# Two projections of a decoder trunk made block by block while scale and shift are still being computed

## The chip, the core and the metric

The kernel runs on one core of a Trainium2 chip. The metric is device time in microseconds; before the change the median of three runs is 1387.54 us (1387.46 to 1388.73). The engines are TensorE (PE, with its weight loads PEld), VectorE (DVE), ScalarE (ACT), GpSimd (POOL) and SyncE (SP, which here only issues transfers). Instructions of one engine run in the order in which the planner has put them.

## The reference, cut to what matters

One decoder layer for 576 tokens (512 of a prompt, 64 of eight samples), 1024 channels. Everything in this document happens in its first lines:

```python
ada = jax.nn.silu(c) @ w_ada + b_ada              # c: 9 rows
sh1, sc1, g1, sh2, sc2, g2 = jnp.split(ada, 6, axis=-1)
xm = x * (1.0 + sc1) + sh1                        # scale and shift, per sequence
proj = xm @ w_in                                  # 1024 -> 9228, cut into branches
u, v, ga, gg, pin, zz, xbc, dtr, gl = jnp.split(proj, IN_SPLIT_IDX, axis=-1)
h = ga * jax.nn.sigmoid(gg)                       # branch B: gate, then a convolution of 31 taps
```

The four branches, a gated merge, two layer norms and a mixture of 32 experts follow; they are not touched.

## The kernel before, in words

All activations lie with channels on partitions: `xT` is 8 blocks of 128 channels by 576 tokens. Products are made in split precision: each fp32 operand is a high part rounded to fp32r and a low part. ScalarE rounds (`cast`, line 316), VectorE subtracts (`lo`, line 322), and `prod` (line 581) makes high x high, high x low and low x high. One projection of 128 columns is 8 blocks x 3 x 2 halves of 288 tokens = 48 matmuls (line 589) into one `mm` tile in PSUM; there are two `mm` tiles.

**Weights.** `plan_front` (line 507) lists every weight tile in the order of use, and `Pipe` loads them in that order on SP's queue into a ring of buffers (`fill`, line 215). A kind `w1` tile (512 KB, for scale and shift) is used as it is; a `ct` tile (512 KB, for one projection) is split when one is asked for by `get` (line 280): `get` splits all that are loaded while fewer than four split ones lie unused. A split carries a high priority (line 257). The first eight `w1` tiles lie in buffers of the split weights, the other eight in buffers of their own (`r0`), the `ct` tiles in four `raw` buffers; so 20 loads are issued at the start, 16 `w1` and four `ct`, and between them, by hooks, the eight blocks of `xT` (288 KB each, after every second `w1`) and the small tensors `prm`.

**Scale and shift** go block by block, here called turns 0 to 7. `rows(k)` (line 427) takes two `w1` tiles and makes scale and shift of block k as nine rows, in 32 matmuls of the profile (line 434); ScalarE copies them to `adr` (line 438). `cols(k)` (line 440) turns them into columns on TensorE (line 446), VectorE adds the bias (line 447), ScalarE scales and shifts the prompt's tokens of the block (line 450), POOL those of the samples, and VectorE makes the high part `xh` (line 453) and the low part `xl` (line 454). `cols` and the copy carry a high priority, so `cols(k)` comes right behind `rows(k)`.

**Branch B** comes next. `b_step(j)` (line 693) makes projection `gg` (`pg`), takes its sigmoid into `sg` on ScalarE (line 704), makes projection `ga` (`pa`), and VectorE multiplies them into `ebp` and `ebs` (lines 706 to 708). From then on the convolution can start: 31 taps of block j on VectorE (line 720), those of the samples on POOL (lines 727 to 732). The taps wait in a list from which `step` takes so many behind each product. `ebp` and `ebs` take up space that `xT` and the other tiles of the start have left.

**The order.** The program says what comes first; a planner (`schedule_with_timeline_sim`) then puts each engine's instructions in order by its own estimate of when they are ready, and among ready ones takes the one with the higher priority, by default the one that was written first. So an instruction may come ahead of earlier ones that wait.

Of the kernel before, what the change touches and what calls it, by code (L numbers as in the profile page):

```python
# [176 lines left out]
NH, NR = 4, 4  # L177
# [13 lines left out]
BME = lambda nc: nc.vector  # L191
HP0 = 2000
N0 = 8
GA = 4
NL = 7
GM = (1, 1, 1, 1, 1)
# [111 lines left out]
class K:  # L308
# [64 lines left out]
    def build(s):  # L373
        nc, A, tc, ctx = s.nc, s.A, s.tc, s.ctx
        s.pse = ExitStack()
        s.ps = s.pse.enter_context(s.pool("ps", space=PSUM))
        con = ctx.enter_context(s.pool("con", side="left"))
        s.con = con
        ring = ctx.enter_context(s.pool("ring", side="left"))
        M = s.M = ExitStack()  # L380
        mp = M.enter_context(s.pool("M", side="left"))
        X = s.X = ExitStack()
        xp = X.enter_context(s.pool("X", side="left"))
        s.cst = con.tile([128, C_N], F32, name="cst")
        s.prm = con.tile([128, P_N], F32, name="prm")
        x0 = ExitStack()
        stp = x0.enter_context(s.pool("start", side="right"))
        cT = stp.tile([128, 8, 9], F32, name="cT")
        bT = stp.tile([128, 16], F32, name="bT")
        nc.scalar.dma_start(cT, A["cT"])  # L390
        nc.scalar.dma_start(bT, A["ba1"])
        nc.scalar.dma_start(s.cst, A["cst"])
        s.plan_front()
        s.ring = ring
        s.pipe = Pipe(s, s.plan, ring, NH, lambda i: (ring, "hi" if i < NH else "lo") if i < 2 * NH else
                      (stp, "r0") if i < 16 else (ring, "raw"), {"raw": NR, "r0": N0, "hi": NH, "lo": NH})
        xT = stp.tile([128, 8, NT], F32, name="xT")
        for k in range(8):
            s.pipe.hook[2 * k + 1] = lambda k=k: nc.sync.dma_start(xT[:, k], A["xT"][:, k])
        s.pipe.hook[16] = lambda: nc.sync.dma_start(s.prm, A["prm"])  # L400
        s.pipe.fill()
        eps = con.tile([128, 1], F32, name="eps")
        nc.vector.memset(eps, EPS)
        s.eps = eps
        s.dram = ctx.enter_context(s.pool("scr", space=bass.MemoryType.DRAM))

        zz = stp.tile([128, 513], F32, name="zz")
        nc.vector.memset(zz, 0.0)
        nc.scalar.activation(zz[:, 512:], eps, AF.Silu)
        p = s.ms()  # L410
        for _ in range(NW):
            nc.tensor.matmul(p[:9], zz[:, :9], zz[:, :512], start=True, stop=True)

        sil = s.sil = con.tile([128, 8, 32], F32, name="sil")
        nc.gpsimd.memset(sil, 0.0)
        nc.scalar.activation(sil[:, :, :9], cT, AF.Silu)
        s.adad = s.dram.tile([9, 4096], F32, name="adad")
        nc.gpsimd.dma_start(s.adad, A["bada"].to_broadcast([9, 4096]))
        b1 = bT.rearrange("p (k v) -> p k v", v=2)[:, :, 0]
        nc.vector.tensor_scalar(b1, b1, 1.0, None, op0=OP.add)  # L420
        scsh = stp.tile([128, 8, 2, 9], F32, name="scsh")
        xh = xp.tile([128, 8, NT], FR, name="xh")
        xl = xp.tile([128, 8, NT], FR, name="xl")
        s.xh, s.xl = xh, xl
        adr = {}

        def rows(k):

            p = s.ms()
            for v in range(2):  # L430
                w = s.pipe.take(2 * k + v)
                for i in range(8):
                    g = 32 * (i % 4)
                    nc.tensor.matmul(p[g:g + 32, v * 128:(v + 1) * 128], sil[:, i], w[:, i * 128:(i + 1) * 128],
                                     start=(i < 4), stop=(i >= 4), skip_group_check=True)
            adr[k] = stp.tile([128, 256], F32, name="adr", tag="adr", bufs=3)
            with tc.high_priority(offset=HP0):
                nc.scalar.copy(adr[k], p[:, :256])

        def cols(k):  # L440

            r = adr.pop(k)
            q = s.ms()[:, :18].rearrange("p (v r) -> p v r", r=9)
            with tc.high_priority(offset=HP0):
                for v in range(2):
                    nc.tensor.matmul(q[:, v], r[:, v * 128:(v + 1) * 128], s.cc("m9"), start=True, stop=True)
                nc.vector.tensor_tensor(scsh[:, k], q, bT[:, 2 * k:2 * k + 2].unsqueeze(2).to_broadcast([128, 2, 9]), OP.add)
                sc, sh = scsh[:, k, 0], scsh[:, k, 1]
                xs = xT[:, k, TP:].rearrange("p (b t) -> p b t", t=8)
                nc.scalar.activation(xT[:, k, :TP], xT[:, k, :TP], AF.Identity, bias=sh[:, 0:1], scale=sc[:, 0:1])  # L450
                nc.gpsimd.tensor_tensor(xs, xs, sc[:, 1:9].unsqueeze(2).to_broadcast([128, 8, 8]), OP.mult)
                nc.gpsimd.tensor_tensor(xs, xs, sh[:, 1:9].unsqueeze(2).to_broadcast([128, 8, 8]), OP.add)
                nc.vector.tensor_copy(xh[:, k, :], xT[:, k, :])
                s.xlast = nc.vector.tensor_tensor(xl[:, k, :], xT[:, k, :], xh[:, k, :].bitcast(F32), OP.subtract)
        for k in range(8):
            rows(k)
            if k:
                cols(k - 1)
        cols(7)
        x0.close()  # L460
        merged = mp.tile([128, 8, NT], F32, name="merged")
        s.merged = merged


        s.stk = []

        def opn(name, side):
            e = ExitStack()
            p = e.enter_context(s.pool(name, side=side))
            s.stk.append(e)  # L470
            return p, e
        s.opn = opn
        s.wk, s.wke = opn("wk", "left")
        s.bp, be = opn("bp", "right")
        s.cp, ce = opn("cp", "right")
        for j in range(4):
            s.b_step(j)
            s.step(7, s.anchor)
        for g in range(4):
            s.c_step(g)  # L480
            s.step(2.0, s.anchor)
        s.gates("C", 2, 4, lambda: s.yC, first=True, budget=6.0)
        ce.close()
        s.yAp, ye = opn("yAp", "left")
        s.ap, ae = opn("ap", "right")
        s.a_u()
        s.a_v()
        s.flush()
        ae.close()
        s.gates("B", 1, 4, lambda: s.yB, budget=6)  # L490
        be.close()
        s.dp1, s.d1e = opn("dp1", "right")
        s.dp, d2e = opn("dp", "right")
        s.dpa, dae = opn("dpa", "right")
        s.d_proj()
        s.flush()
        dae.close()
        s.dpb, dbe = opn("dpb", "right")
        s.ssd_queue()
        s.gates("A", 0, 4, lambda: s.yA, budget=BA)  # L500
        s.cond_rows()
        ye.close()
        if any(fn is None for c, fn, a in s.bg):
            s.flush(True)
        s.de = (dbe, d2e)

    def plan_front(s):
        A = s.A
        pl = []
        for i in range(16):  # L510
            pl.append(("w1", A["wa1"][i], 1024))
        for i in range(12):
            pl.append(("ct", A["wct"][i], 1024))

        def gates(k, w, kt):
# [32 lines left out]
        def add(nm, ap):  # L548
            if len(s.mi) == GA:
                s.wag = len(pl)  # L550
# [27 lines left out]
                               start=(hs[0] == 0), stop=(hs[0] > 0), skip_group_check=True)  # L578
        return p

    def prod(s, p, wh, wl, off, kt, h, l, m=128):

        nc = s.nc
        for k in range(kt):
            a, b = wh[:, off + k * m:off + (k + 1) * m], wl[:, off + k * m:off + (k + 1) * m]
            for n, (w, x) in enumerate(((a, h), (a, l), (b, h))):
                for hf in range(2):
                    xk = x[k] if isinstance(x, list) else x[:, k]
                    nc.tensor.matmul(p[:m, hf, :288], w, xk[:, hf * 288:(hf + 1) * 288],  # L589
                                     start=(k == 0 and n == 0), stop=(k == kt - 1 and n == 2))  # L590

    def ctile(s):
        wh, wl = s.pipe.get("ct")
        p = s.mm()
        s.prod(p, wh, wl, 0, 8, s.xh, s.xl)
        return p
# [676 lines left out]
    def build2(s):  # L1273
# [72 lines left out]
        for i in range(base, len(s.plan)):  # L1346
            m = s.mi.get(i, -1)
            if m < 0 or len(seq) < GA:
                t = (s.ring, "raw") if n9 % (NR + NB) < NR else (s.raw2, "rb")
                n9 += 1  # L1350
                if seq and m < 0:
                    late.append(t)
            elif len(seq) < GA + len(late):
                t = late[len(seq) - GA]
            else:
                t = seq[-(GA + len(late))]
            tags[i] = t
# [662 lines left out]
```

## Time and profile before

| | us |
|---|---|
| median of three runs | 1387.54 |
| the profiled execution, its own time | 1388.56 |
| its span, first to last instruction | 1386.7 |
| TensorE busy | 1309.0 |
| VectorE busy | 776.7 |
| ScalarE busy | 408.8 |
| GpSimd busy | 320.4 |

The profile is one execution. Times in it are counted from the first instruction. A line of the timeline gives start and duration in us, engine, line of the kernel, operation, output <- inputs with shape, how many were merged (xN), and in brackets how long the engine was idle before and what ended that. A matmul's duration overlaps that of its neighbours, so the pace is read from starts. PEclk is the clock that TensorE was granted, as a share of 2.4 GHz.

### The profile page before, as it was taken

Reading aid. Unit: us, or ns where it says so; the run is one execution under the profiler, and the core shown is the slowest. Engines: PE = TensorE matmul, PEld = TensorE weight load, DVE = VectorE, ACT = ScalarE, POOL = GpSimd, SP = SyncE. Lnnn points to the kernel's source line nnn. Section 1 sums busy time; section 2 is a strip of 40 time slices with the busy share of each in tenths; the row PEclk is TensorE's granted clock in tenths of the full one; section 3 lists DMA queues with packets and bytes.
Section 4 is the critical chain, followed back from the end, with each engine's and each line's share of the span. In section 5 each row is a group of like instructions: output and inputs, shape, how many; then the busy total and the mean of one; then the engine's idle time right before and its main releaser. Section 6 shows DMA issues by size and latency. Waiting matters only on the chain. (4 is left out here: it accounts for less than half of the span.)

```text
span 1386.7 us, 20311 instructions
## 1 busy us (share of the span) xinstructions
PE 1309.0 (94%) x7962; PEld 944.1 (68%) x7962; DVE 776.7 (56%) x1333; ACT 408.8 (29%) x657; POOL 320.4 (23%) x335
## 2 busy tenths in 40 slices
PE   7997899999999999999999987999999999999992
PEld 5997899999999877788899863344334444444331
DVE  3799797572676356667524487244444334434347
ACT  3311222642463424556422332021111111111114
POOL 1796004051321315333333151000000000000003
PEclk6998999999999989899999997999999999999997
DMA  9522123222322354361222969899999999999972
GB/s 378 151 76 61 54 92 110 69 69 84 108 77 84 113 200 170 129 230 43 72 85 93 320 241 358 340 414 414 414 415 414 415 413 415 414 415 415 415 296 99
DMA packets 90376, 318.15 MB, mean 229 GB/s; under 512 B 11113, under 2 KB 11265, under 8 KB 90271
## 3 DMA queue, kind: packets, MB, share of 16 engines
q1 hardware_dynamic: 83176, 293.29, 55.6%
q0 software_dynamic: 6528, 22.63, 4.8%
q8 instruction: 63, 1.03, 0.3%
q10 hardware_dynamic: 576, 0.93, 0.2%
q14 instruction: 33, 0.27, 0.1%
HBM read 307.16 MB, written 9.78 MB: 229 GB/s over the span
## 5 line engine op out<-in xcount | busy, mean ns | idle before, releaser
L1746 PE MATMUL mh<-raw,xg 128*64 128x512 f32 x1024 | 247.7, 605 | 0.2 <-DMA raw<-in_we_dram 0.2
L589 PE MATMUL mm<-xh,wh 128*128 128x288 f32 x1088 | 244.0, 305 | 2.9 <-DVE ebs L708 2.4
L589 PE MATMUL mm<-xh,wl 128*128 128x288 f32 x1088 | 240.4, 302 | 2.1 <-DVE wl L322 2.1
L589 PE MATMUL mm<-xl,wh 128*128 128x288 f32 x1088 | 240.4, 301 | 0.0
L316 ACT CAST wh<-raw 128x1024 fp32r<-128x1024 f32 (+3 forms) x120 | 113.1, 948 | 316.5 <-PE mm L589 228.3
L322 DVE TENSOR_TENSOR wl<-raw,wh 128x1024 fp32r<-128x1024 f32 (+3 forms) x112 | 133.3, 1194 | 130.1 <-ACT wh L316 129.7
L589 PEld LDWEIGHTS mm<-xh,wh 128*128 128x128 f32 x1088 | 180.9, 194 | 5.7 <-issue 3.3
L589 PEld LDWEIGHTS mm<-xh,wl 128*128 128x128 f32 x1088 | 178.8, 192 | 4.8 <-DVE wl L322 3.2
L589 PEld LDWEIGHTS mm<-xl,wh 128*128 128x128 f32 x1088 | 179.2, 193 | 0.4 <-issue 0.3
L1746 PEld LDWEIGHTS mh<-raw,xg 128*64 128x64 f32 x1024 | 75.2, 138 | 132.8 <-issue 117.4
L1793 DVE TENSOR_TENSOR x<-x,mc 128x512 f32<-128x512 f32 x120 | 78.2, 682 | 124.3 <-PE mc L1732 124.3
L1703 PE MATMUL mh<-raw,h 128*64 128x512 f32 x512 | 130.2, 601 | 1.0 <-ACT h L1761 0.7
L1670 POOL DMA_INDIRECT gr<-xmd,idi x16 | 16.2, 1010 | 415.9 <-PE mh L1746 385.4
L720 DVE SCALAR_TENSOR_TENSOR acc<-ebp,prm,acc 128x512 f32<-128x512 f32 x120 | 104.9, 883 | 2.1
L1703 PEld LDWEIGHTS mh<-raw,h 128*64 128x64 f32 x512 | 40.4, 136 | 72.0 <-issue 56.6
L1715 ACT CAST yh<-y 128x512 fp32r<-128x512 f32 x32 | 19.8, 620 | 220.9 <-DVE y L1714 207.4
L632 POOL TENSOR_TENSOR merged<-merged,sg 128x576 f32<-128x576 f32 x23 | 43.2, 1877 | 108.9 <-DVE sg L631 108.8
L1714 DVE SCALAR_TENSOR_TENSOR y<-mh,ws,G 128x512 f32<-128x512 f32 x32 | 24.0, 751 | 70.2 <-PE mh L1703 70.2
L1732 PEld LDWEIGHTS mc<-yh,ohT 128*128 128x128 f32 x120 | 22.4, 187 | 52.1 <-issue 47.1
L1732 PE MATMUL mc<-yh,ohT 128*128 128x512 f32 x120 | 53.6, 447 | 0.0
L1750 ACT ACTIVATE sg<-mh 128x512 f32<-128x512 f32 x16 | 9.6, 597 | 128.5 <-issue 78.6
L1732 PE MATMUL mc<-yl,ohT 128*128 128x512 f32 x120 | 47.4, 395 | 0.0
(436 smaller groups left out, 2010.3 us busy)
## 6 DMA issues: line engine op xcount, KB each, us to landing
raw<-in_we_dram SPq DMA_DIRECT2D x384, 512.0 KB
raw<-in_wa_dram SPq DMA_DIRECT2D x48, 512.0 KB
raw<-in_wct_dram SPq DMA_DIRECT2D x36, 512.0 KB
raw<-in_wgl_dram SPq DMA_DIRECT2D x32, 512.0 KB
raw<-in_wo_dram SPq DMA_DIRECT2D x16, 512.0 KB
raw<-in_wbr_dram SPq DMA_DIRECT2D x24, 256.0 KB
s<-in_st_ssm_dram POOLq DMA_DIRECT2D x4, 768.0 KB, 4.8
out_ssms_dram<-s POOLq DMA_DIRECT2D x4, 768.0 KB, 4.7
```

Of the source, the lines that this page charges most:

```text
L316: r = s.nc.scalar.copy(out, in_)
L322: r = (s.nc.gpsimd if pool else s.nc.vector).tensor_tensor(out, full, hi, OP.subtract)
L589: nc.tensor.matmul(p[:m, hf, :288], w, xk[:, hf * 288:(hf + 1) * 288], start=(k == 0 and n == 0), stop=(k == kt - 1 and n == 2))
L632: (nc.vector if nm == "D" and d == 7 else nc.gpsimd).tensor_tensor(m, m, sg, OP.add)
L720: nc.vector.scalar_tensor_tensor(o, i, wt, o, op0=OP.mult, op1=OP.add)
L1670: s.glast = nc.gpsimd.indirect_dma_start(out=gr[:n], out_offset=None, in_=s.xmd[:, :], in_offset=bass.IndirectOffsetOnAxis(ap=ix[:n, 0:1], ...
L1703: s.dlast = s.pe(nc.tensor.matmul(p[r], h[:, f, r], ws[o][:, kk * 512:(kk + 1) * 512], start=(f == 0), stop=(f == 3), skip_group_check=True))
L1714: V.scalar_tensor_tensor(y, p, ws, s.G2[0][:, hf * 512:hf * 512 + 512], op0=OP.mult, op1=OP.mult)
L1715: nc.scalar.copy(yh, y)
L1732: m = pe(s.nc.tensor.matmul(p[:r], oT[:n, t * 128:t * 128 + r], y[:n, hf], start=(i == 0), stop=(i == 1)))
L1746: s.pe(nc.tensor.matmul(p[o * 64:o * 64 + 64], xg(k, o), ws[o][:, kk * 512:(kk + 1) * 512], start=(k == 0), stop=(k == 7), skip_group_chec ...
L1793: nc.vector.tensor_tensor(o, o, p[:n], OP.add)
```

## The change

Four edits. The first two `ct` tiles stand in the plan behind the eighth `w1` tile instead of behind all sixteen (`E0`); `s.w1` holds the places of the `w1` tiles. The hooks for `xT` follow the `w1` tiles, and that of `prm` stands behind the third `ct` tile. `prod` takes a list of blocks. And a new function `first(z)` makes the products of both projections for the blocks up to z: behind `rows(5)` and `cols(4)` those of blocks 0 and 1, behind turn 6 and 7 two blocks more each (`FK`), behind `cols(7)` the last two. `ctile` hands out the two finished `mm` tiles to `b_step(0)`. The number of matmuls, loads, casts and subtractions is the same.

```diff
+E0 = 8
+FK = {5: 2, 6: 4, 7: 6}
...
-                      (stp, "r0") if i < 16 else (ring, "raw"), {"raw": NR, "r0": N0, "hi": NH, "lo": NH})
+                      (stp, "r0") if i < 18 and s.plan[i][0] == "w1" else (ring, "raw"), {"raw": NR, "r0": N0, "hi": NH, "lo": NH})
...
-            s.pipe.hook[2 * k + 1] = lambda k=k: nc.sync.dma_start(xT[:, k], A["xT"][:, k])
-        s.pipe.hook[16] = lambda: nc.sync.dma_start(s.prm, A["prm"])
+            s.pipe.hook[s.w1[2 * k + 1]] = lambda k=k: nc.sync.dma_start(xT[:, k], A["xT"][:, k])
+        s.pipe.hook[18] = lambda: nc.sync.dma_start(s.prm, A["prm"])
...
-                w = s.pipe.take(2 * k + v)
+                w = s.pipe.take(s.w1[2 * k + v])
...
+        pre = []
+
+        def first(z):
+            if not pre:
+                pre.extend((s.mm(),) + s.pipe.get("ct") for _ in range(2))
+                s.kdone = 0
+            for k in range(s.kdone, z):
+                for p, wh, wl in pre:
+                    s.prod(p, wh, wl, 0, 8, xh, xl, ks=[k])
+            s.kdone = z
         for k in range(8):
             rows(k)
             if k:
                 cols(k - 1)
+            if k in FK:
+                first(FK[k])
         cols(7)
+        first(8)
+        s.pre = [p for p, _, _ in pre]
...
+        s.w1 = []
         for i in range(16):
+            if i == E0:
+                for j in range(2):
+                    pl.append(("ct", A["wct"][j], 1024))
+            s.w1.append(len(pl))
             pl.append(("w1", A["wa1"][i], 1024))
-        for i in range(12):
+        for i in range(2, 12):
             pl.append(("ct", A["wct"][i], 1024))
...
-    def prod(s, p, wh, wl, off, kt, h, l, m=128):
+    def prod(s, p, wh, wl, off, kt, h, l, m=128, ks=None):
...
-        for k in range(kt):
+        for k in ks or range(kt):
...
     def ctile(s):
+        if s.pre:
+            return s.pre.pop(0)
         wh, wl = s.pipe.get("ct")
```

## Rows read from the trace of the kernel before

**Rows 1.** The page, busy time of each engine: us, share of the span, instructions.

```profile
PE 1309.0 (94%) x7962; PEld 944.1 (68%) x7962; DVE 776.7 (56%) x1333; ACT 408.8 (29%) x657; POOL 320.4 (23%) x335
```

**Rows 2.** Timeline, one turn of scale and shift.

```profile
24.82 2.32 PE L434 MATMUL ms<-raw,sil 128*32 128x128 f32 x32
...
26.86 0.37 ACT L438 COPY adr<-ms 128x256 f32<-128x256 f32 x1 [0.91 <-PE ms L434]
...
27.28 1.02 PE L446 MATMUL ms<-cst,adr 128*128 128x9 f32 x4
...
28.24 2.22 PE L434 MATMUL ms<-raw,sil 128*32 128x128 f32 x32
```

**Rows 3.** Stretches: length, TensorE busy (instructions), granted clock, DMA share, GB/s.

```profile
97.20:100.30 3.10, 3.10 (x13) 0.50 0.02 5
100.30:102.00 1.70, 1.70 (x15) 0.99 0.25 94
...
129.80:134.40 4.60, 4.60 (x15) 0.50 0.12 13
...
35.10:38.80 3.70, 3.54 (x14) 0.50 0.52 168
38.80:40.00 1.20, 1.20 (x11) 0.96 0.37 150
14.00:34.00 20.00, 19.04 (x213) 0.50 1.03 405
```

**Rows 4.** Timeline, first matmuls of turns 2 and 4; DMA issues, size.

```profile
13.01 0.61 PE L434 MATMUL ms<-raw,sil 128*32 128x128 f32 x2 [1.46 <-DMA raw<-in_wa_dram]
...
19.88 0.18 PEld L434 LDWEIGHTS ms<-raw,sil 128*32 128x32 f32 x2 [0.54 <-DVE xh L453]
...
xT<-in_xT_dram SPq DMA_DIRECT2D x8, 288.0 KB
```

**Rows 5.** Timeline, the first projection, at both clock levels.

```profile
35.07 0.85 PE L589 MATMUL mm<-xh,wh 128*128 128x288 f32 x2
...
35.28 1.22 DVE L322 TENSOR_TENSOR wl<-raw,wh 128x1024 fp32r<-128x1024 f32 x1
...
37.20 0.68 PE L589 MATMUL mm<-xh,wh 128*128 128x288 f32 x2
...
37.68 0.68 PE L589 MATMUL mm<-xl,wh 128*128 128x288 f32 x2
...
42.22 0.42 PE L589 MATMUL mm<-xl,wh 128*128 128x288 f32 x2
...
42.48 0.43 PE L589 MATMUL mm<-xh,wl 128*128 128x288 f32 x2
```

**Rows 6.** Timeline, from the first projection's end to the second gating product.

```profile
43.48 1.05 ACT L316 CAST wh<-raw 128x1024 fp32r<-128x1024 f32 x1 [4.44 <-PE mm L589]
...
44.55 1.28 ACT L704 ACT_TABLE_LOAD   x1
...
45.84 0.65 ACT L704 ACTIVATE sg<-mm 128x576 f32<-128x576 f32 x1
...
50.17 0.46 DVE L706 TENSOR_TENSOR ebp<-mm,sg 128x288 f32<-128x288 f32 x1 [4.38 <-PE mm L589]
...
51.72 1.63 DVE L322 TENSOR_TENSOR wl<-raw,wh 128x1024 fp32r<-128x1024 f32 x1
...
65.26 0.45 DVE L706 TENSOR_TENSOR ebp<-mm,sg 128x288 f32<-128x288 f32 x1
```

**Rows 7.** A stretch with each engine's busy time; timeline, TensorE's and POOL's waits.

```profile
60.00:70.00 10.00, 10.00 (x77) 10.00 (x77) 9.89 (x12) 2.14 (x3) 9.37 (x9) 1.00 0.17 54
...
97.18 0.82 PE L589 MATMUL mm<-xh,wh 128*128 128x288 f32 x2 [2.40 <-DVE ebs L708]
...
144.39 1.95 PE L868 MATMUL mm<-mx,poolw 128*128 128x288 f32 x4 [3.95 <-DVE mx L861]
...
164.07 2.48 POOL L773 TENSOR_TENSOR rs<-acc 128x576 f32<-128x576 f32 x1 [34.19 <-DVE acc L720]
```

## The prediction

> **What bounds the kernel now.** I read the page first, for the share of each engine, then the start in order of time, because the whole change lies in its first 50 us. TensorE is busy for 94% of the span [rows 1], so the question is where it is late or slow. The reader should see four things in order.
>
> First, the turns of scale and shift. A turn is 30 matmuls of one block's `w1` tiles, the copy `adr`, four matmuls that turn rows into columns, and the next turn starts 3.42 us after the last (28.24 - 24.82) [rows 2]. Nothing in that turn waits for a transfer: about 2.0 us of matmuls, 0.5 for the copy, 1.0 for the columns. But the weights come no faster: those of turn 2 are waited for at 13.01, those of turn 4 are there at 19.88, so 3.43 us a turn [rows 4]. Chain and transfers set nearly the same pace. TensorE is busy for 19.04 of 20 us there, at a granted clock of 0.50, the 1.2 GHz level [rows 3].
>
> Second, the first projections start at 35.07, still at 0.50; the clock is at the 2.4 GHz level only from about 38.8, some 3.7 us later [rows 3, 5]. A pair of their matmuls takes 0.48 us before (37.68 - 37.20) and 0.265 after (two from 42.22 and two from 42.48) [rows 5]: 0.24 and 0.133 each, a factor of 1.8.
>
> Third, the handover. When the first projection is done ScalarE casts the next weights (43.48, 1.05), loads a table (44.55, 1.28) and only then does the sigmoid (45.84, 0.65). All of that hides under the second projection, and VectorE starts the gating product `ebp` at 50.17 [rows 6].
>
> Fourth, from 50 to 144 VectorE is the limit: 9.89 of 10 us busy, and TensorE stands still for it at 97.18 and, the last time, at 144.39 [rows 7]. So only what brings `ebp` forward, or takes VectorE's work out of that stretch, moves the end. After 144 TensorE is fed again and everything moves as one.
>
> **The change, part by part.** The profiled execution took 1388.56 us (span 1386.7, 1.9 outside it), 1.0 above the median of 1387.54. The sum is made on the trace, and its difference is taken from the median.
>
> *Transfers.* The same 20 loads are issued at once, in another order: two of 512 KB pass ahead of eight `w1` tiles and four blocks of `xT` on SP's queue. A turn's two tiles and one block of 288 KB are 1.34 MB in 3.43 us [rows 4], 0.392 MB/us, so 1.05 MB delays turn 4 and all later ones by 2.7 us: the weights of turn 4 are there at 22.6 instead of 19.88. `prm` stays where it was in bytes. The next four loads wait for the splits of the first four, as before; those behind the first two are issued earlier, after the old end of the queue, and cost nothing.
>
> *Casts and subtractions.* Two casts (1.05) and two subtractions (1.22) [rows 5, 6] move from 34 to 37 into the turns. The turns leave ScalarE 2 and VectorE 2 of each 3.4 us, so they hide. If a cast stands in front of an `adr` or an `xT` activation it costs up to 1.05 on that turn's chain; TensorE then has products to do, so I take 0, bounds 0 to 1.
>
> *Products.* No matmul is added. From the end of turn 3's columns, at 21.5, TensorE has four turns of 2.1 + 1.0 and 96 products of 0.24, at the half clock 12.5 + 23.0 = 35.5 us. It can go on at about 22.2: the first conv weights take the place of turn 4's in the queue (19.9), plus 1.05 and 1.22. From there TensorE is never without work, if the planner puts the products into the waits. If T is the time at which the clock rises, the two projections end at E = T + (35.5 - (T - 22.2))/1.78 + 0.35 = 32.8 + 0.438 T. The 1.78 is 1.8 for products and a little less for turns, the 0.35 is what the same sum lacks for the kernel before (49.8 against 50.17). Last block: its channels are ready some 4 us after its turn, under the 36 products still left.
>
> *T* is the unknown. In this trace the clock rose 3.1 to 4.6 us after products began or came back (97.2 to 100.3, 129.8 to 134.4) and 3.7 in this place [rows 3]; turns alone never raised it in 20 us. Products begin between 22.2 and 29 (behind turn 5), so T lies between 25.3 and 33.6 if turns in between do no harm. I take 32, near the late end because of the turns: E = 46.8, 3.4 us ahead of 50.17.
>
> *What is late next.* Both projections now end together and both hold their accumulators (there are two), so the sigmoid is no longer hidden. The cast of the fifth weights is free some 1.0 before E, when the first projection has read its weights for the last time; it and that of the sixth carry the planner's priority, the sigmoid doesn't. So ScalarE does cast, cast, table, sigmoid: E - 1.0 + 1.05 + 1.05 + 1.28 + 0.65 = E + 3.05, and `ebp` starts at E + 3.1 = 49.9, hardly earlier than 50.17. TensorE stands still for those 3 us, and queued behind it is all its work.
>
> *What is won in the wait.* VectorE subtracts the fifth and the sixth weights in it; the sixth cost 1.63 at 51.72, inside the busy stretch [rows 6]. So from one `ebp` to the next, 15.09 before (65.26 - 50.17), VectorE needs 13.5. TensorE needs 96 x 0.133 = 12.75, and after such a gap the clock is at 0.50 for about 3.1 us (97.2 to 100.3, after a stop of 2.4) [rows 3, 7], some 1.5 more: 14.3. The second `ebp` comes at E + 3.1 + 14.35 = 64.25, against 65.26: **1.0 us earlier**, or 15.0 - 0.438 T in general. If ScalarE does the sigmoid first, `ebp` starts at E + 0.1, but the fifth subtraction (about 1.7) falls into the stretch: E + 16.9, so 1.5 earlier. The order matters for half a microsecond only.
>
> The trace has the table load end at 45.83 and the sigmoid start at 45.84 [rows 6]. The Trainium skill's ScalarE: Activation LUTs, What ACT_TABLE_LOAD costs, puts some 1.38 us of drain on top of the load's 1.28; by that the gain would be -0.4 and the time 1387.9. The trace decides against it.
>
> *POOL.* `ebs` and its four loads take the place of `xT` in SBUF and wait for its last read, which now comes just ahead of the last products, so the sample taps on POOL start up to 8 us later. POOL has 34.19 us of slack at 164.07 [rows 7]: nothing.
>
> Sum: 1387.54 - 1.0 = **1386.5**.
>
> **Rivals.**
>
> *Faster by more than 0.2%.* The planner fills the waits from 22.2 on and the clock rises by 26: E = 44.2, gain 3.6, with the sigmoid first 4.1: 1383.4 to 1383.9. For it: products are ready from 22, and the clock once rose 3.1 after products came back. Against it: until 30 two thirds of TensorE's work are turns. It decides at T below 28.
>
> *Slower.* The clock stays at the half level while turns and products alternate, as it stays there through all turns before. Products of blocks 0 to 3 lie among the turns, so up to 22.2 + 12.5 + 48 x 0.24 = 46.2 nothing is dense, T = 50, E = 54.7, loss 6.9: 1394.4. It decides at T above 40.6. Against it: 24 products stand together, 5.8 us at the half clock, longer than each of the rises above took. A rule of the Trainium skill speaks for it: TensorE: Matmul & The Clock Gate, Why this matters for your kernels, wants thin products looped over all blocks of the contraction before the next load, or the clock swings at every block. No row here has such a mix.
>
> *Given back.* The planner keeps all products behind turn 5. TensorE then waits some 2.6 us for late weights, T is 34, E = 32.8 + 14.9 + 2.6/1.78 = 49.1, and the sigmoid's 3 us eat it: 1.3 slower, 1388.8, no change that can be measured. For it: the order in the program says so, and what has been written first goes first.
>
> **How the numbers follow.** A measurement of this kernel can tell about 0.2% from no change, 2.8 us: below 1384.8 is faster, above 1390.3 slower. Forecast 0.44 (own range 1385 to 1388), faster rival 0.25, slower rival 0.10, given back 0.21, of which 0.02 beyond 0.2% (a cast ahead of a turn's copy on top). So faster 0.25, same 0.63, slower 0.12. The range goes from 1383.0 (the faster rival with the sigmoid first) to 1390.4, and leaves out the slower rival and little else.
>
> **What would show it.** In the profile after: turn 4 some 2.7 us later; the clock at 2.4 GHz from about 32; the 96 products done near 46.8; ScalarE with two casts, the table and the sigmoid behind them; TensorE idle for about 3 us until that sigmoid, then half clock for some 3 us; first `ebp` near 49.9 and second near 64.3; the wait for `mx` that ends at 144.39 ending near 143.4, and the same distance at the end. The forecast is wrong if the clock rises before 28 or after 40, if TensorE goes on after E without a wait and the stretch shrinks by more than 1.6, or if VectorE is not what fixes 144.39.

## The result, and the profile after

The changed kernel takes 1402.71 us (median of 4 runs, 1399.84 to 1405.02), the kernel before in the same series 1387.5 (4 runs): a ratio of 1.0098, interval 1.0072 to 1.0124. It is 15 us slower. Ratios and medians are those of the fast runs (one of `b_late2`, 2483.65 us, is not among them), and a ratio is not just the quotient of two medians, here 1.0110. The forecast was 1386.5, the range ended at 1390.4. The profiled execution took 1402.56 us. Its busy times hardly differ from [rows 1]: TensorE is busy for 4.1 us more in a span 13.9 us longer, with the same number of instructions, so most of the loss is idle time.

```profile
PE 1313.1 (94%) x7962; PEld 944.9 (67%) x7962; DVE 779.7 (56%) x1333; ACT 408.5 (29%) x657; POOL 319.7 (23%) x335
```

**The front came out about as forecast, and a little better.** Timeline of the kernel after, the mix (turn 4 begins at 25.91, behind products), the handover and the second `ebp`; beside [rows 4 to 6]:

```profile
21.01 0.85 PE L612 MATMUL mm<-xh,wh 128*128 128x288 f32 x2 [1.48 <-ACT wh L318]
...
25.91 0.41 PE L436 MATMUL ms<-raw,sil 128*32 128x128 f32 x2
...
43.87 0.80 PE L612 MATMUL mm<-xh,wh 128*128 128x288 f32 x4 [1.40 <-DVE xh L455]
...
45.24 1.05 ACT L318 CAST wh<-raw 128x1024 fp32r<-128x1024 f32 x1 [2.72 <-PE mm L612]
...
46.30 1.28 ACT L729 ACT_TABLE_LOAD   x1
...
47.60 0.65 ACT L729 ACTIVATE sg<-mm 128x576 f32<-128x576 f32 x1
48.14 1.04 ACT L318 CAST wh<-raw 128x1024 fp32r<-128x1024 f32 x1
48.28 0.46 DVE L731 TENSOR_TENSOR ebp<-mm,sg 128x288 f32<-128x288 f32 x1 [0.74 <-ACT sg L729]
...
48.30 0.68 PE L612 MATMUL mm<-xh,wh 128*128 128x288 f32 x2 [2.31 <-ACT sg L729]
...
62.97 0.46 DVE L731 TENSOR_TENSOR ebp<-mm,sg 128x288 f32<-128x288 f32 x1 [1.36 <-PE mm L612]
```

The first product is at 21.01, the projections end at 46.0, TensorE stands still 2.31 us for the sigmoid, and `ebp` comes at 48.28 (50.17 before) and 62.97 (65.26 before). The clock, by stretch (columns as in [rows 3], each with TensorE, weight loads, VectorE, ScalarE and GpSimd busy):

```profile
20.00:24.00 4.00, 2.99 (x11) 2.71 (x12) 2.53 (x3) 2.00 (x3) 0.00 (x0) 0.50 1.04 408
24.00:34.00 10.00, 10.00 (x128) 8.47 (x126) 2.79 (x6) 2.26 (x4) 1.18 (x4) 0.97 1.03 405
34.00:44.00 10.00, 8.60 (x98) 7.43 (x98) 5.80 (x11) 4.86 (x7) 2.69 (x6) 1.00 0.59 223
48.00:52.00 4.00, 3.70 (x16) 3.70 (x17) 3.60 (x7) 1.18 (x2) 4.00 (x9) 0.57 0.98 245
```

From 24.8 on it stays at the 2.4 GHz level (0.97 to 1.00) while turns and products alternate; from 48 to 52, behind the stop, it is 0.57 on average.

**GpSimd is late.** Its timeline after, first the loads, then the taps:

```profile
44.84 0.20 POOL L723 MEMSET ebp<- 128x120 f32 x1 [1.52 <-DVE xl L456]
45.37 3.63 POOL L725 DMA_DIRECT2D ebs<-in_st_conv_dram  x4 [0.32 <-issue]
...
52.30 0.93 POOL L769 DMA_DIRECT2D out_convs_dram<-ebs  x1
53.20 0.67 POOL L752 TENSOR_TENSOR acc<-ebs,prm 128x256 f32<-128x256 f32 x1
...
64.15 0.91 POOL L769 DMA_DIRECT2D out_convs_dram<-ebs  x1 [6.93 <-DVE ebs L733]
...
139.25 1.06 POOL L757 TENSOR_TENSOR acc<-acc,ct 128x256 f32<-128x256 f32 x1
```

and before:

```profile
38.54 0.20 POOL L698 MEMSET ebp<- 128x120 f32 x1 [1.52 <-DVE xl L454]
...
50.28 0.63 POOL L727 TENSOR_TENSOR acc<-ebs,prm 128x256 f32<-128x256 f32 x1 [4.25 <-issue]
...
127.71 0.72 POOL L732 TENSOR_TENSOR acc<-acc,ct 128x256 f32<-128x256 f32 x1
```

The loads follow the last `xl`, 6.3 us later than before, and a transfer out of the conv state, put among the taps, holds all of GpSimd for 6.93 us until VectorE has written the `ebs` it reads. So the taps, which start 2.9 us later, end at 140.3 instead of 128.4. What that does to VectorE's small sums, after and then before:

```profile
128.41 0.65 DVE L877 TENSOR_TENSOR sb<-sb 128x64 f32<-128x64 f32 x1
...
130.79 0.82 DVE L883 SCALAR_TENSOR_TENSOR mx<-sb,es 128x64 f32<-128x64 f32 x1
...
145.88 2.26 PE L893 MATMUL mm<-mx,poolw 128*128 128x288 f32 x4 [5.50 <-DVE mx L886]
```

```profile
131.67 0.21 DVE L852 TENSOR_TENSOR sb<-sb 128x64 f32<-128x64 f32 x1
...
133.07 0.21 DVE L858 SCALAR_TENSOR_TENSOR mx<-sb,es 128x64 f32<-128x64 f32 x1
```

The same 64 columns take 0.21 us when GpSimd is through and 0.65 to 0.82 while it works. The lead of 3.9 us that VectorE had at 118 us (the same sum at 115.72 and, before, at 119.58) is gone: the wait for `mx` ends at 145.88 instead of 144.39 [rows 7].

**And a second loss, far behind.** From 150 to 485 us the two traces run in step, the changed kernel about 1 us behind, with the same order on every engine. From 490 on the planner has put the instructions of TensorE, VectorE, ScalarE and GpSimd in another order, and by 685 us the lag behind the first trace of the kernel before has grown to 13. From there to the end it changes little.

### The profile page after: what moved, and what is told of

Read it like the earlier page. It is cut to its first block, busy times and chain, and to the rows that moved or that the text cites. A ratio compares the mean times of both kernels' runs of the same rounds, so it can differ in the third digit from the quotient of the medians.

```text
span 1400.6 us, 20312 instructions
## 1 busy us (share of the span) xinstructions
PE 1313.1 (94%) x7962; PEld 944.9 (67%) x7962; DVE 779.7 (56%) x1333; ACT 408.5 (29%) x657; POOL 319.7 (23%) x335
## 5 line engine op out<-in xcount | busy, mean ns | idle before, releaser
L745 DVE SCALAR_TENSOR_TENSOR acc<-ebp,prm,acc 128x512 f32<-128x512 f32 x120 | 102.0, 859 | 2.2
L656 DVE TENSOR_TENSOR sg<-mm,sg 128x576 f32<-128x576 f32 x24 | 18.1, 756 | 53.8 <-PE mm L612 53.7
```

Source lines behind the costliest of these rows:

```text
L656: a = nc.vector.tensor_tensor(sg, q[:, :, :288], sg, OP.mult)
L745: nc.vector.scalar_tensor_tensor(o, i, wt, o, op0=OP.mult, op1=OP.add)
```

## The experiments

**How an order was held.** For each engine the instructions of a stretch are listed in one kernel's order, and each is queued behind the one ahead of it (`PINS` holds the list). This ties no engine to another, adds no wait, and leaves the work as it is:

```diff
+def pin(tc):
+    ...
+    for e, (at, steps) in PINS.items():
+        last = q[e][at]
+        for d in steps:
+            at += d
+            i = q[e][at]
+            tc.add_manual_dep(i, last.name, mybir.DependencyInfo(mybir.DependencyClass.NoSync, mybir.DependencyReason.DATA),
+                              reason="pin")
+            last = i
...
         k.pse.close()
+        pin(tc)
```

**All runs together.** Times in us from the traces: first and second `ebp`, end of the sample taps, end of TensorE's last wait for `mx`, which VectorE makes for the pooling; then TensorE's lag at 485, 600 and 685 us behind the second trace of the kernel before (`b_again`); then the median time and the ratio to the kernel before in the same series, with its interval.

```
          ebp 1   ebp 2   taps    mx      485    600    685   median   ratio
before    50.17   65.26  128.43  144.39   0.4    1.8    1.8   1387.5   1
b_again   50.87   65.90  128.24  144.51   0      0      0     1389.1   (one run)
after     48.28   62.97  140.32  145.88   1.2   14.2   14.6   1402.7   1.0098 [1.0072, 1.0124]
p_late    49.08   63.74  141.16  146.73   2.5    6.4    9.3   1394.4   1.0036 [1.0011, 1.0060]
p_all     49.47   63.24  136.13  144.57   0.4    0.9    3.7   1389.3   1.0008 [0.9979, 1.0036]
b_late    51.39   65.96  127.48  143.76  -0.4   10.9   11.3   1399.2   1.0070 [1.0043, 1.0097]
b_late2   50.57   65.42  128.69  144.64  -0.8   11.9   12.5   1394.4   1.0044 [1.0014, 1.0073]
b_pool    50.32   63.04  140.44  146.00   1.7    5.6    5.6   1391.9   1.0025 [1.0004, 1.0046]
a_early   53.94   70.09  125.97  144.93   0.6    1.2    5.5   1389.3   1.0013 [0.9991, 1.0035]
b_early   53.77   68.61  122.70  141.65  -2.9   -1.6   -1.6   1388.1   1.0010 [0.9988, 1.0033]
a_mid     49.54   64.24  131.33  141.72  -2.9    3.0    7.3   1387.0   0.9979 [0.9959, 1.0000]
b_mid     50.71   64.03  121.13  138.68  -6.8   -3.6   -3.7   1385.4   0.9973 [0.9950, 0.9997]
a_behind  55.04   69.70  129.67  146.55   2.3    2.6    2.6   1390.0   1.0007 [0.9989, 1.0025]
a_notap   49.41   62.52   55.02  125.87 -19.7  -20.1  -20.1   1366.7   (one run)
```

Single runs of the kernel before lay between 1377.8 and 1400.0, and the intervals are some 0.2 to 0.3% to either side. The columns up to `mx` are much steadier: 144.39 and 144.51 for the kernel before. Up to 485 us a trace keeps the lag that it has at `mx`, within about 1 us. Between 485 and 685 us it may not, even in the old order: there `b_pool` falls 3.9 us further behind, `a_mid` 10.2, `a_behind` 0.3. `b_pool`, `p_late` and `a_mid` were profiled in executions well above their medians (1397.55, 1401.43 and 1394.72 us). So what an order costs is read from the medians, not from one trace's lag. The lag at 600 is that of one matmul, and in `after`, `b_late` and `b_late2` that matmul stands at another place in the order.

**1. `p_late`: the change, the old order from 150 us on.** (Two exchanges stayed as in the changed kernel, a tap at 147 us and two copies of ScalarE near 493.) 

> The changed kernel, with the order of the instructions on TensorE, VectorE, ScalarE and GpSimd held to that of the kernel before from about 150 us on; the first 150 us are the changed kernel's own. Theory A (what is lost between 490 and 680 us is the other order that the planner wrote there): the trace is 1.4 us behind the kernel before at 485 us, and that stays; 1389 us. Rival R (the loss there is a real consequence of the new front: later buffers, transfers, clock): about 1401 us, as the changed kernel.

The ratio falls from 1.0098 to 1.0036: the order from 490 on is worth 0.6%, some 8.6 us. It was to be 1389 and is 1394.4, so that expectation missed: more remains than the lag at 485 says.

**2. `b_late`: the kernel before, the changed kernel's order from 150 us on.** 

> The kernel before, unchanged to 150 us, with the changed kernel's order from there on. Theory A: 10 to 12 us lost between 490 and 680 us without any of the change: 1398 to 1399 us. Rival R: 1387 to 1388 us, the order costs nothing by itself.

1399.2, ratio 1.0070: nothing of the change is in this kernel but the later order, and it loses 9.8 us on its series' median of 1389.4. So the order alone is shown to cost 0.4 to 1.0%, the interval of its ratio.

**3. `b_late2`: only the second half of that order, 585 to 680 us.** 

> The kernel before with only the later half of the changed kernel's order, from about 585 to 680 us; the part from 490 to 530 us is its own. If the cost of the order lies there (TensorE at half clock near 590 and 610 us and a wait of 6.3 us instead of 3.3 for GpSimd's xs at 668 us): 5 to 8 us lost, 1393 to 1397 us. Rival (it begins with the waits of VectorE's s at 494 us, and all later steps follow from them): 1387 to 1389 us.

1394.4, ratio 1.0044, 6.7 us on 1387.7: by the medians most of the price lies here, though the intervals of this ratio and of `b_late`'s overlap. TensorE's last wait of the stretch, in `b_late`, `b_late2`, the kernel before again, and `p_late`:

```profile
684.34 2.29 PE L755 MATMUL mm<-xs,cst 128*128 128x288 f32 x4 [6.31 <-POOL xs L1301]
```

```profile
685.52 2.29 PE L755 MATMUL mm<-xs,cst 128*128 128x288 f32 x4 [6.29 <-POOL xs L1301]
```

```profile
674.19 1.24 PE L752 MATMUL mm<-xs,cst 128*128 128x288 f32 x4 [3.33 <-POOL xs L1298]
```

```profile
682.25 2.29 PE L780 MATMUL mm<-xs,cst 128*128 128x288 f32 x4 [3.33 <-POOL xs L1326]
```

The wait is 3.0 us longer, and that belongs to the order: it is 6.29 to 6.31 in all three kernels with the new one and 3.33 in all others but `a_notap`, ten traces. The four matmuls behind it take 2.29 instead of 1.24, at a granted clock of 0.50 instead of 0.99. That is not the order's alone: in `p_late`, `p_all`, `a_early` and `a_mid` they take 2.29 too, behind the short wait.

**4. `b_pool`: the kernel before, only GpSimd's order from 50 to 140 us as after.** 

> The kernel before with one thing of the changed kernel, GpSimd's order of taps and transfers from 50 to 140 us; all else in its own order. Theory P: a stall of GpSimd behind the transfer out, later taps beside VectorE's sums, 3 to 6 us lost by 148 us: 1390 to 1393 us. Against P (the 5 us came from elsewhere): 1387 to 1388 us.

1391.9, ratio 1.0025. The stall comes with the order, and so does the late `mx`:

```profile
64.22 0.92 POOL L747 DMA_DIRECT2D out_convs_dram<-ebs  x1 [6.63 <-DVE ebs L711]
```

```profile
146.00 1.30 PE L871 MATMUL mm<-mx,poolw 128*128 128x288 f32 x2 [5.50 <-DVE mx L864]
```

By `mx` only 1.5 us are lost (146.00 against 144.51); the rest of the 0.25% lies behind it and isn't located. A surprise is in the table: this kernel has the second `ebp` at 63.04, as early as the changed one, with none of its front. While GpSimd stands, VectorE is quick: four taps take 3.11 us from 58.50 on in the changed kernel, six 7.15 from 53.27 on in the kernel before. So the 2.3 us that the second `ebp` had won in the changed kernel need not come from its front: a GpSimd that stands lends them, and takes them back from 118 on. (`p_all` has 63.24 without the stall, but its taps start 4.6 us later than before.)

**5. `p_all`: the change, the old order everywhere behind the front.** 

> The changed kernel with the order of the kernel before from the first sigmoid on, GpSimd's out transfers of the conv state among its sample taps included. Theory A with theory P (GpSimd standing 6.93 us behind a transfer out, and its taps then running beside VectorE's work until 140 us, turned a lead of 4.3 us at 118 us into a lag of 1.5 us): the lead of the front stays, 2 to 4 us: 1384 to 1385 us. If GpSimd's order is not the cause of that part: 1389 us. Rival R: about 1400 us.

1389.3, ratio 1.0008, not the 1384 to 1385 of theory A with theory P. With both other orders undone, the change alone is worth nothing that can be measured; the expected lead of 2 to 4 us isn't there. The transfers out are back in their old places, but the taps start at 54.87 and end at 136.13, because their state still loads behind the last block, and `mx` comes at 144.57 as ever.

**6. `a_notap`: the price of the sharing.** Sample taps 1 to 30 are left out of GpSimd's work.

```diff
         def taps_s(t):
+            if t:
+                return
```

> The changed kernel held to the old order on TensorE, VectorE and ScalarE, with all sample taps but the first left out of GpSimd's work (the convolution of the sample rows is then not computed): the price of the sharing by itself. Theory P: VectorE's taps take 0.75 us instead of 1.00 throughout, its sums 0.2 to 0.3 us instead of 0.6 to 0.8, and the wait for mx ends 10 us or more earlier, near 130 to 134 us. Rival (VectorE's operations are long for another reason, or TensorE bounds this stretch): within 3 us of 144.6.

VectorE's taps, `a_notap` and then `p_all`: min/median/max ns, first and last start.

```profile
L748 DVE SCALAR_TENSOR_TENSOR acc<-ebp,prm,acc x55: 739/751/1144, 52.1 to 129.3; 128x512 f32<-128x512 f32 x55
```

```profile
L748 DVE SCALAR_TENSOR_TENSOR acc<-ebp,prm,acc x54: 736/1000/1619, 52.1 to 145.9; 128x512 f32<-128x512 f32 x54
```

0.75 against 1.00 us, and the wait for `mx` ends at 125.87, 18.7 us earlier and well ahead of the 130 to 134 expected: far more than the change was ever about. The other way round it shows too. GpSimd's sums of line 451 in the kernel before (min/median/max ns), and the last of the eight:

```profile
L451 POOL TENSOR_TENSOR xT<-xT,scsh x8: 296/297/1208, 11.1 to 35.4; 128x64 f32<-128x64 f32 x8
```

```profile
35.44 1.21 POOL L451 TENSOR_TENSOR xT<-xT,scsh 128x64 f32<-128x64 f32 x1 [2.75 <-DVE scsh L447]
```

Seven take 0.30 us. The last starts 0.16 us after VectorE's subtraction of `wl` [rows 5], takes 1.21 and ends 0.15 us behind it. The Trainium skill gives a reason in SBUF — State Buffer, SBUF: two separate sides: a GpSimd operation that reads SBUF and a VectorE operation with two inputs there need the same pair of ports, and whichever starts first holds it for its whole instruction. The rows agree: the sum of 0.30 waits out the subtraction, and a VectorE sum of 0.21 takes 0.65 to 0.82 beside taps of about 1.0.

**7 and 8. `a_early` and `b_early`: the state loads first of all, with the change and without.** The convolution's buffers get a pool beneath the one of the start, the taps follow GpSimd's last sum of x, the transfers out follow the last tap; the other engines keep the old order.

```diff
+        cv = s.cve.enter_context(s.pool("cv", side="right"))
+        s.ebp = cv.tile([128, 4, 542], F32, name="ebp")
+        s.ebs = cv.tile([128, 4, 8, 38], F32, name="ebs")
+        s.acc = cv.tile([128, 4, NT], F32, name="acc")
+        s.ct = cv.tile([128, 4, 8, 8], F32, name="ct")
         x0 = ExitStack()
...
+                    with s.tc.issue_after(s.ltap.ins):
+                        nc.gpsimd.dma_start(A["convs"][:, jj], s.ebs[:, jj, :, 8:38])
```

> The changed kernel with the order of the kernel before held on TensorE, VectorE and ScalarE from the first sigmoid on, and, beyond that, the buffers of the convolution (its state, its input, its sum and the scratch of the sample taps) in a pool of their own, so that their loads need not wait for the last block of x; the taps follow GpSimd's last sum of x, the transfers out follow the last tap. Theory P (what ate the lead between 118 and 148 us is GpSimd's taps, which end 7 us later than before and until then lengthen VectorE's small sums): taps start near 45 us and end by 131 us, VectorE's sums at 127 to 136 us are short again, the wait for mx ends 2.5 to 3 us before 144.39; 1384.5 to 1386 us, ratio 0.997 to 0.999. Rival (the lead is lost to something else between 118 and 148 us, the granted clock for one): the wait for mx ends at 144.4 to 145.6 as in the kernel with all of the old order, ratio 1.000 to 1.001.

> The kernel before with the same early buffers, the same place of taps and transfers out. Theory P: the taps start near 38 us instead of 50.28 and end some 8 us sooner, near 122 us; VectorE is slowed by them between 38 and 50 us, where it has time to spare, and no more between 122 and 130 us: 1 to 3 us gained, 1385 to 1386.5 us, so that the change adds on top of it 1 us or less. Rival (only the change's own later taps matter): 1387.5 us.

Both missed, it seems for one reason: the loads, now at 2.12 us, cost the front its weights. Transfers of the first 20 us, `a_early` and then `p_all`:

```profile
DMA packets 2284, 6.23 MB, mean 311 GB/s; under 512 B 566, under 2 KB 566, under 8 KB 2275
```

```profile
DMA packets 2525, 7.17 MB, mean 359 GB/s; under 512 B 550, under 2 KB 550, under 8 KB 2515
```

The first `ebp` falls back by 4.5 us (`a_early` against `p_all`) and 2.9 (`b_early` against `b_again`). But most of that (`a_early`) or more than that (`b_early`) is won back by `mx`: in `b_early` VectorE is 2.9 us late at 52 and 2.9 early at 136.

**9 and 10. `a_mid` and `b_mid`: the loads behind the weights.** As 7 and 8, with three loads between GpSimd's last two sums of x, the fourth behind them, and the loads for the pooling after seven taps.

```diff
+                for jj in {6: (0, 1, 2), 7: (3,)}.get(k, ()):
+                    with tc.issue_after(s.xslast.ins):
+                        nc.gpsimd.dma_start(s.ebs[:, jj, :, 0:30], A["st_conv"][:, jj])
```

> The changed kernel with the old order on TensorE, VectorE and ScalarE from the first sigmoid on; the convolution's buffers in their own pool, its four state loads issued between and behind GpSimd's last two sums of x (not in the first microseconds, where they held up the weights by 3.5 us), the loads for the pooling only after seven of the sample taps, the transfers out after the last tap. Theory P: front as in the kernel held to the old order (first ebp at 48 to 50 us), taps from about 46 us to 128 us, VectorE's sums short from 128 us on, the wait for mx ends near 141 us (before 144.39); 1384 us, ratio 0.996 to 0.998. Rival (the sharing only moves: each microsecond that the taps run earlier is paid by VectorE's longer operations there): mx at 144 to 145 us, ratio 1.000 to 1.001.

> The kernel before with the same loads and the same place of taps. Theory P: state loads at 33 to 37 us, taps from about 38 us, end near 120 us, first ebp still at 50 to 51 us; mx at 140 to 141 us; 1384 us, ratio 0.996 to 0.998; the change itself then adds nothing to it. Rival (sharing only moves): mx at 144 us, ratio 1.000.

Up to `mx` both came as theory P had it: 141.72 and, 1.3 us earlier than expected, 138.68. The ratios are 0.9979 and 0.9973, and the medians, 1387.0 and 1385.4, are later than the 1384 expected. GpSimd in `b_mid`, then in `a_mid`:

```profile
32.59 2.97 POOL L464 DMA_DIRECT2D ebs<-in_st_conv_dram  x3
...
42.17 0.61 POOL L739 TENSOR_TENSOR acc<-ebs,prm 128x256 f32<-128x256 f32 x1 [4.34 <-DMA ebs<-in_st_conv_dram]
```

```profile
40.17 2.97 POOL L466 DMA_DIRECT2D ebs<-in_st_conv_dram  x3
...
49.79 0.63 POOL L764 TENSOR_TENSOR acc<-ebs,prm 128x256 f32<-128x256 f32 x1 [4.22 <-DMA ebs<-in_st_conv_dram]
```

`b_mid` is the version that beats both kernels, by a little (its interval ends at 0.9997), and it does without the change. Between the two, only the change differs: it brings the first `ebp` 1.2 us forward and the taps 7.6 us back, and `mx` comes 3.0 us later. The early pair says the same: 3.3 us. The medians don't tell the two apart.

**11. `a_behind`: the earlier transfers without the mix.** The 96 products stay behind the last block; TensorE and all that follows keep the old order.

```diff
-        first(8)
+        with tc.issue_after(s.clast.ins):
+            first(8)
```

> The changed kernel's earlier transfers alone: the weights of the first two projections still come amid those of scale and shift, but their 96 products stay behind the last block, in the order of the kernel before, as does all that follows on the four engines. Theory (what the change gives is that the products fill the waits of turns 3 to 7; the transfers by themselves only make the front 7.5 us longer): the first ebp comes 7 to 8 us after that of the kernel held to the old order (49.47), near 57 us, the clock stays at half until the products; 1392 to 1396 us, ratio 1.004 to 1.006. Rival (the products would find room anyway behind the last block, at full clock): first ebp by 52 us, 1388 to 1390 us.

The first `ebp` is at 55.04, 5.6 us behind `p_all`; that was to be 7 to 8. GpSimd's last sums of x, `a_behind` and then `p_all`:

```profile
39.44 0.29 POOL L457 TENSOR_TENSOR xT<-xT,scsh 128x64 f32<-128x64 f32 x1
```

```profile
44.22 0.30 POOL L457 TENSOR_TENSOR xT<-xT,scsh 128x64 f32<-128x64 f32 x1
```

The last one of the kernel before is at 36.73: the transfers cost 2.7 us, the mix 4.8 more. And 5.6 us of lead at the first `ebp` have shrunk to 2.0 at `mx` (144.57 against 146.55), since the taps begin 4.5 us later in the kernel that mixes. The ratios are the same, 1.0007 and 1.0008, so the 1392 to 1396 expected missed too: the theory had the front's loss right in kind, and left out that GpSimd starts earlier in this kernel.

**12. `b_again`.** 

> The kernel before once more, as the yardstick on the chip of these runs: 1383 to 1399 us in single runs. If the differences of 1 to 3 us that appear after 829 us between kernels of one order are the granted clock's and not the order's, this trace shows such steps against the first trace of the same kernel too.

1389.1; the yardstick of the table. The first trace of the same kernel is 0.4 us behind it at 485, 1.8 at 685 and 0.2 ahead at 900, so steps of that size there say nothing of a kernel. Steps as large as `a_mid`'s between 485 and 685 this pair doesn't show.

## Why the prediction was wrong, step by step

- *Transfers*: right. In `a_behind`, where no products stand in front, turn 4 waits for its weights until 22.59 (22.6 was forecast) and the last block is 2.7 us later (39.44 against 36.73).
- *Products, T and E*: right in the sum, and that in part by luck. The clock was up at 24.8 instead of 32, before the 28 that the prediction had named as a sign against itself and for its faster rival; its formula then gives E = 43.7. The products ended at 46.0, near the 46.8 forecast, because TensorE was not "never without work": among its waits it stood 1.40 us for the last block's `xh` (43.87), which was to hide under the products left. The slower rival's mechanism (a clock that stays at half in the mix) is refuted: the granted clock was 0.97 to 1.00 through turns and thin products alike. The swing that the Trainium skill warns of, in TensorE: Matmul & The Clock Gate, Why this matters for your kernels, no row here shows.
- *What is late next*: right in kind. Table and sigmoid stand free, TensorE waits 2.31 us. The order was cast, table, sigmoid, cast: `ebp` at 48.28 instead of 49.9.
- *What is won in the wait*: from one `ebp` to the next 14.69 us (62.97 - 48.28) instead of 14.35, and TensorE, not VectorE, ended it (1.36), as forecast. So 2.3 us were won at the second `ebp` instead of 1.0, but `b_pool` has as much from the stall alone.
- *POOL*: **the first step that failed.** The sample taps were to "start up to 8 us later", and the 34.19 us of slack made that worth "nothing". The bound held (they start 2.9 us later, 4.6 in `p_all`), and the slack was beside the point. A late GpSimd costs by its company: its 80 us of taps slow VectorE wherever they lie, and the later end of them falls on small sums that suffer most, right ahead of `mx`. With the stall behind the transfer out, which the prediction did not have, they end 11.9 us later. Price: 0.25 to 0.3% (`b_pool`; `p_late` less `p_all`), some 3.5 to 4 us, of which 1.5 and 2.2 are there by `mx`. The longer `wl` of [rows 6], 1.63 beside GpSimd's taps against the 1.22 of [rows 5], could have shown it.
- *"After 144 everything moves as one"*: **the second, and the larger.** Up to 485 us it did: the changed kernel is 1.4 us behind `b_again` at `mx` and 1.2 at 485. From 490 on the program itself is another. The planner's order between 490 and 680 us changed with the front, and costs 0.6 to 0.7% by itself, 8.6 to 9.8 us.
- *The sum*: from `after` to `p_late`, to `p_all` and to the kernel before, the ratio falls by 0.62, 0.28 and 0.08%: the later order, GpSimd's, and all the rest. `b_late` (0.70) and `b_pool` (0.25) give the first two from the other side; each is good to some 0.2 to 0.3%. No rival had either cause. (A turn has 32 matmuls of its `w1` tiles [rows 2], not 30; nothing hangs on it.)

What stays open: why the planner's order turned (its own estimates decide, no trace shows them); how the 9 us divide, beyond the 3.0 us of the wait in experiment 3; and why some executions of kernels in the old order lose several us between 485 and 685 (`a_mid` 10.2, `a_behind` 0.3).

## What to carry to other kernels

Where a planner orders the program, an edit at the start may reorder work half a millisecond later: compare the order of each engine's instructions before you explain a time, and hold the old order to see what the edit itself is worth. Slack of an engine is no proof that it may run late; ask whom it slows while it works, and move it to where that one is idle. A transfer in an in-order queue waits with everything behind it (6.93 us here): put transfers out behind the work they were queued among.

## What had not been expected of the hardware

GpSimd's sample taps cost this kernel 18.7 us at `mx` and about 20 at the end (1366.7 without them, one run). Four loads of 120-byte runs issued at 2 us took the transfers of the first 20 us from 359 to 311 GB/s and held the weights up by 3.5 us (the first weights' subtraction at 24.48 instead of 20.99). And the runs of one kernel, the one before, spread by 1.6%.
